# Bias tables of the neighbourhood attention: laid out on the host and loaded by one plain transfer

## The chip, the cores and the metric

The kernel runs on one core of a Trainium2 chip. The metric is device time in microseconds (us) of one execution, as the median of several runs. Engines: PE multiplies matrices (PEld loads its stationary operand), DVE and ACT work on vectors, POOL (GpSimd) does small vector work and issues some transfers, SP issues most transfers.

## The reference, cut to what matters

Three layers over 256 tokens of width 1024: an attention layer with an MLP, a retention layer with an MLP, and a hybrid attention layer. The first layer has eight heads of window attention (a) and eight of neighbourhood attention (b). Tokens form 4 rows of 64 columns; a query sees, in every row, 16 columns around its own, with a bias per head, row distance and column distance:

```
cstart = jnp.clip(qc - kw // 2, 0, GRID_W - kw)
col_valid = (kc[None, :] >= cstart[:, None]) & (kc[None, :] < cstart[:, None] + kw)
col_idx = jnp.clip(kc[None, :] - qc[:, None] + NA_KW - 1, 0, 2 * NA_KW - 2)
...
bias = rpb_f[:, row_idx[None, :, None], col_idx[:, None, :]]
s = jnp.where(col_valid[:, None, :], s + bias, -jnp.inf)
```

## The kernel before, in words

All weights stream from HBM once, in 1 MB pieces on SP's queue. Each is split into two fp32r parts: ACT copies the rounded part (whi, L246), DVE subtracts it (wlo, L251), and PE multiplies three times. The activations are split in the same way.

The order of instructions on every engine is written by a planner that runs while the kernel is built. The code consists of tasks (generators). Each operation names its engine and an estimated cost; a task goes on when its engine, its inputs and its buffers are free by these estimates, and among the tasks that are ready the one of the lowest priority number is first. The real engines then run their instructions in that order and wait on semaphores for each other. So a step that is taken out of one engine's plan can move other steps, if they stood behind it.

The stage in question is the first attention layer (`_even`, from about 10 to 120 us). Its projections are five panels, qa, ka, qb, kb and vb, of 48 matmuls each. Between the matmuls of a panel lie the heads (`even_head`): PE makes 128x256 scores of two halves; DVE adds a table and takes the row minimum in a custom instruction (L273); ACT takes exponentials (L246); DVE adds the sink to the denominator (den, L251), inverts it (L288) and scales p (tensor_scalar, L259); PE transposes p (L336); ACT and DVE split the result (ph, pl); PE multiplies by v (PV).

The eight (a) heads use a table that DVE makes for each from distances in the tile conste (tab, L259). The eight (b) heads use the tile tb: 128 partitions (2 grid rows x 64 query columns) by 8 heads by 6 rows by 64 key columns. A head for token half t reads 256 of the 384 columns, from 128 - 128t.

tb is filled by the task `bias_tables`, spawned with a delay of 30 (BIAS) and low priority (5). Two transfers on POOL's queue (`pdma`, L302, planned at 1.04 each) read the host's rows, which are repeated 64 times in HBM, with a pitch of one element less than a row, so that partition q gets the row shifted by q. That makes 6144 runs of 64 floats. Columns outside the window then hold other values, and four POOL additions (`ptt`, L293) of 128x768 elements add a mask of 0 and -1e30, which came with conste. The plan gives each 0.0021 us per element and 0.1. At the end the task fires the event "tb", for which the planner holds back head 8, the first (b) head; that head also waits for the panels qb, kb and vb. Other work on POOL in this stage is the inverse square root as a power (`rsqrt`, L298) of st (the norms of q and k heads), r and rm.

Tiles of the stage come from two pools (`Pools`): those whose size is a multiple of 512 bytes from one, the others from the second. conste has 448 columns (1792 bytes), and lies in the second.

Of the kernel before, what the change touches and what calls it, by code (L numbers as in the profile page):

```python
# [11 lines left out]
ALU = mybir.AluOpType  # L12
# [3 lines left out]
P = 128  # L16
# [5 lines left out]
NEG = -1e30  # L22
# [6 lines left out]


K_ID, K_CM, K_CC, K_SS, K_MAIN = 0, 128, 384, 512, 640
K_DIST, K_WM, K_EVEN = 640, 1024, 1088
K_DPOS, K_DNEG, N_CONST = 1088, 1472, 1856

A_ORDER = [0, 4, 1, 5, 2, 6, 3, 7]

# [1 line left out]
def vap(ap, dims):  # L38

    return bass.AP(ap.tensor, ap.offset, [ap.ap[0]] + [list(d) for d in dims])  # L40
# [24 lines left out]
class Kernel:  # L65
# [801 lines left out]
    def _even(self, pool):  # L867
        nc, aps, cols = self.nc, self.aps, self.cols
        self.res["qn"] = 2
        self.hb = self.EB  # L870
        const = pool.tile([P, K_EVEN - K_MAIN], F32, name="conste")
        nc.sync.dma_start(const, aps["const"][:, K_MAIN:K_EVEN])
        dist, wmask = const[:, K_DIST - K_MAIN:K_DIST - K_MAIN + 384], const[:, K_WM - K_MAIN:K_WM - K_MAIN + 64]

        gg = pool.tile([P, 2], F32, name="gg")
        for i, (cq, ck) in enumerate(((C_QA, C_KA), (C_QB, C_KB))):
# [3 lines left out]
        tb = pool.tile([P, 8, 6 * 64], F32, name="tb")  # L880

        def bias_tables():

            rp = aps["rpb"]
            for r2 in range(2):
                src = bass.AP(rp.tensor, rp.offset + r2 * 48 * 64 * P + 63, [[P - 1, 64], [64 * P, 48], [1, 64]])
                self.pdma(tb[r2 * 64:(r2 + 1) * 64].rearrange("p h (j k) -> p (h j) k", k=64), src)
            yield 15.0
            wm = vap(wmask, [[0, 12], [1, 64]])
            for h in range(0, 8, 2):  # L890
                tv = tb[:, h:h + 2].rearrange("p h (j k) -> p (h j) k", k=64)
                yield from self.ptt(tv, tv, wm, ALU.add)
            self.fire("tb", at=self._last(self.ready, tb, "T"))
        self.spawn(bias_tables(), self.BIAS, self.LOW)

        def qk_norm(ps, t, nh):
# [737 lines left out]
def _pack(w, panels, kmajor=False):  # L1634

    kt = w.shape[0] // P
    blocks = []
    idx = [(c, g) for c in range(len(panels)) for g in range(kt // 4)]
    if kmajor:
        idx = [(c, g) for g in range(kt // 4) for c in range(len(panels))]  # L1640
    for c, g in idx:
        a, b = panels[c]
        blk = w[g * 512:(g + 1) * 512, a:b].reshape(4, P, b - a).transpose(1, 0, 2)
        blocks.append(np.ascontiguousarray(blk).reshape(-1))
    return np.concatenate(blocks)


def _uniform(n, w=512):
    return [(i, i + w) for i in range(0, n, w)]


def _columns(v):
    return np.ascontiguousarray(np.asarray(v).reshape(-1, P).T)


def _constants():
    c = np.zeros((P, N_CONST), np.float32)
    p = np.arange(P)[:, None]
    c[:, K_ID:K_ID + P] = np.eye(P)
    d = np.abs(np.arange(384)[None, :] - P - p)  # L1660
    c[:, K_DIST:K_DIST + 384] = np.where(d <= 128, d, 1e30)
    c[:, K_CM + P:K_CM + 2 * P] = np.where(np.arange(P)[None, :] <= p, 0.0, NEG)
    qc = p % 64
    st = np.clip(qc - 8, 0, 48)
    kc = np.arange(64)[None, :]
    c[:, K_WM:K_WM + 64] = np.where((kc >= st) & (kc < st + 16), 0.0, NEG)
    diff = np.arange(384)[None, :] - P - p
    c[:, K_DPOS:K_DPOS + 384] = np.maximum(diff, 0)
    c[:, K_DNEG:K_DNEG + 384] = np.maximum(-diff, 0)
    inv = np.power(np.float32(10000.0), -np.arange(32, dtype=np.float32) * np.float32(2.0) / np.float32(64))  # L1670
    for t in range(NT):
        ang = ((p + t * P).astype(np.float32) * inv[None, :].astype(np.float32)).astype(np.float64)
        co, si = np.cos(ang), np.sin(ang)
        c[:, K_CC + t * 64:K_CC + (t + 1) * 64] = np.concatenate([co, co], 1)
        c[:, K_SS + t * 64:K_SS + (t + 1) * 64] = np.concatenate([-si, si], 1)
    return c


def _layout(inputs):
    i = {k: np.asarray(v) for k, v in inputs.items()}  # L1680
    f = {}
    f["x"] = i["x"][0]
    f["mem"] = i["mem_2"][0]
    cols = np.zeros((P, N_COLS), np.float32)
    for base, v in ((G_ATTN, i["attn_norm_e"][0]), (G_MLP0, i["mlp_norm"][0]), (G_MLP1, i["mlp_norm"][1]),
                    (G_RET, i["ret_norm_o"][0]), (G_GN, i["ret_gn_o"][0]), (G_IN, i["g_in_2"][0]),
                    (G_MEM, i["g_mem_2"][0])):
        t = _columns(v)
        cols[:, base:base + t.shape[1]] = t
    for base, n in ((C_QA, "q_norm_a"), (C_KA, "k_norm_a"), (C_QB, "q_norm_b"), (C_KB, "k_norm_b")):  # L1690
        cols[:, base] = np.tile(i[n][0], 2)
    cols[:, C_SINK:C_SINK + 8] = i["sink_a"][0][None, :]
    cols[:, C_DEC:C_DEC + 8] = i["decay_fwd_o"][0][None, :]
    cols[:, C_DEC + 8:C_DEC + 16] = i["decay_bwd_o"][0][None, :]
    f["cols"] = cols
    f["const"] = _constants()
    rpb = np.zeros((2, 8, 6, P), np.float32)
    for r2 in range(2):
        rpb[r2, :, :, 48:79] = i["rpb_b"][0][:, 5 - r2:11 - r2, :]
    f["rpb"] = np.tile(rpb, 64)  # L1700
    w = i["w_in_e"][0]
    qa = w[:, :512].reshape(D, 8, 64)[:, A_ORDER].reshape(D, 512)
    f["w_in_e"] = _pack(np.concatenate([qa, w[:, 512:]], 1),
                        [(0, 512), (512, 768), (768, 1280), (1280, 1792), (1792, 2304)])
    wo = i["w_out_e"][0]
    oa = wo[:512].reshape(8, 64, D)[A_ORDER].reshape(512, D)
    f["w_out_e"] = _pack(np.concatenate([oa, wo[512:]], 0), _uniform(D), kmajor=True)
    w = i["w_in_o"][0]
    parts = []
    for hp in range(4):  # L1710
        parts += [w[:, hp * 256:(hp + 1) * 256], w[:, D + hp * 256:D + (hp + 1) * 256],
                  w[:, 2 * D + hp * 512:2 * D + (hp + 1) * 512], w[:, 4 * D + hp * 512:4 * D + (hp + 1) * 512]]
    f["w_in_o"] = _pack(np.concatenate(parts, 1), _uniform(6 * D))
    f["w_out_o"] = _pack(i["w_out_o"][0], _uniform(D), kmajor=True)
    for l in range(2):
        f[f"w_mlp_in{l}"] = _pack(i["w_mlp_in"][l], _uniform(4 * D))
        f[f"w_mlp_out{l}"] = _pack(i["w_mlp_out"][l], _uniform(D), kmajor=True)
    f["w_mem"] = _pack(i["w_mem_kv_2"][0], _uniform(D))
    w = i["w_in_2"][0]
    MQ, MK, MV, MG, DQ, DK, DV, DG, IQ, IK, XQ, XG, GL = (0, 512, 1024, 1536, 2048, 2560, 3072, 3584, 4096, 4608,  # L1720
                                                         4680, 5192, 5704)
    full = lambda o: (o, o + 512)
    f["w_in_2"] = _pack(w, [full(IQ), (IK, IK + 328), (XQ + 256, XQ + 512), full(XG), full(MQ), full(MK), full(MV),
                            full(GL + 2048), full(GL + 2560), full(DQ), full(DK), full(DV), full(MG),
                            full(GL), full(GL + 512), full(DG), full(GL + 1024), full(GL + 1536)])
    f["b_merge"] = i["b_merge_2"][0]
    f["w_up"] = np.concatenate([_pack(i[n][0], _uniform(D)) for n in ("w_up_cross_2", "w_up_moba_2", "w_up_dsa_2")])
    f["w_out_2"] = _pack(i["w_out_2"][0], _uniform(D), kmajor=True)
    f["g_final"] = i["g_final_2"]
    return {k: np.ascontiguousarray(v, dtype=np.float32) for k, v in f.items()}  # L1730
# [20 lines left out]
```

## Time and profile before

| | us |
|---|---|
| median of 3 runs | 1014.18 (1013.54 to 1014.5) |
| the profiled execution | 1014.55 |
| its span | 1012.8 |

| engine | busy us | share of the span |
|---|---|---|
| PE | 1000.0 | 99% |
| PEld | 860.1 | 85% |
| DVE | 689.5 | 68% |
| ACT | 536.1 | 53% |
| POOL | 39.5 | 4% |

The span begins with the first instruction and ends with the last. An engine is busy while an instruction of its own lies on it; an instruction that is held by something else counts as busy too. PE's ends are modelled, so starts are the better measure there. The granted clock is the share of full speed that the chip allowed PE: 1.0 is 2.4 GHz, 0.5 is 1.2 GHz. A row of the order of time gives start, length, engine, line, operation, the tiles (out<-in), the shape and the count; a bracket at its end gives the idle time before it and what ended that.

### The profile page before, as it was taken

To read this page: it belongs to the slowest core of one execution; us is meant where nothing else is said; L and a number is where in the kernel's file an instruction comes from. 1 tells how busy PE (TensorE), PEld (TensorE's weight loads), DVE (VectorE), ACT (ScalarE), POOL (GpSimd) and SP (SyncE) were. 2 spreads that over 40 slices of the span, in tenths; PEclk is the share of its full clock that TensorE was granted. 3 is DMA by queue.
4 is the path that set the end of the run, shared out by engine and by line. 5 is a ranking of instruction groups with operands and counts; after the bars stand their busy time and mean duration, and the time that the engine had idled before them with its cause. 6 is when DMAs were issued, how large, how long until landed. Compare 5 with 4: busy or idle time off the path is not lost.

```text
span 1012.8 us, 14238 instructions
## 1 busy us (share of the span) xinstructions
PE 1000.0 (99%) x5602; PEld 860.1 (85%) x5602; DVE 689.5 (68%) x1133; ACT 536.1 (53%) x817; POOL 39.5 (4%) x44
## 2 busy tenths in 40 slices
PE   9989999999999999999999999999999999999997
PEld 7878889999998888888889999998878788888885
DVE  6997667555556977777667545556769756576774
ACT  7766646444445655656446444445554553454453
POOL 1340000000000000000000000000100000000000
PEclk9989999999999999999999999999999999999999
DMA  9734245555554544443545555553625435543531
GB/s 333 231 112 159 84 166 203 178 202 182 197 204 153 195 166 155 172 171 129 205 166 191 187 206 172 203 207 112 213 83 172 161 136 195 193 172 128 195 125 42
DMA packets 27108, 173.66 MB, mean 171 GB/s; under 512 B 3168, under 2 KB 3424, under 8 KB 7584
## 3 DMA queue, kind: packets, MB, share of 16 engines
q1 hardware_dynamic: 25344, 168.05, 47.2%
q0 software_dynamic: 1120, 4.06, 1.7%
q8 instruction: 44, 0.72, 0.3%
q10 hardware_dynamic: 576, 0.64, 0.2%
q14 instruction: 24, 0.20, 0.1%
HBM read 171.69 MB, written 1.05 MB: 171 GB/s over the span
## 4 chain that ended last, share of the span: by engine, by line
PE 95%; DVE 2%; DMA 1%; ACT 1%; issue 0%; POOLq 0%; ACTq 0%; DVEq 0%
PE bank L326 91%; PE bank L336 4%; DMA x<-in_x 1%; DVE p L273 1%; DVE tab L259 0%; DMA cols<-in_cols 0%; ACT p L246 0%; DVE pl L251 0%; DVE p L259 0%; DVE den L251 0%; DVE wlo L251 0%; DVE st L283 0%; DVE qn L251 0%; ACT whi L246 0%; ACT nraw L246 0%
## 5 line engine op out<-in xcount | busy, mean ns | idle before, releaser
L251 DVE TENSOR_TENSOR wlo<-raw,whi 128x1024 fp32r<-128x1024 f32 (+1 forms) x324 | 384.9, 1191 | 187.9 <-ACT whi L246 183.0
L246 ACT ACTIVATE whi<-raw 128x1024 fp32r<-128x1024 f32 (+1 forms) x324 | 333.3, 1032 | 239.5 <-PE bank L326 233.8
L326 PE MATMUL bank<-whi,xT 128*128 128x512 f32 (+2 forms) x1184 | 378.7, 390 | 0.7 <-ACT whi L246 0.4
L326 PEld LDWEIGHTS bank<-whi,xT 128*128 128x128 f32 x1184 | 221.1, 189 | 45.7 <-issue 3.0
L326 PE MATMUL bank<-wlo,xT 128*128 128x512 f32 (+2 forms) x592 | 227.1, 384 | 0.0
L326 PE MATMUL bank<-xT,whi 128*128 128x256 f32 x1024 | 182.1, 280 | 0.0
L326 PEld LDWEIGHTS bank<-xT,whi 128*128 128x128 f32 x1024 | 157.3, 187 | 1.1
L326 PE MATMUL bank<-xT,wlo 128*128 128x256 f32 x512 | 142.9, 279 | 0.0
L326 PEld LDWEIGHTS bank<-wlo,xT 128*128 128x128 f32 x592 | 112.0, 189 | 18.8
L326 PE MATMUL bank<-whi,hh 128*128 128x512 f32 x256 | 100.3, 392 | 0.0
L326 PE MATMUL bank<-whi,hl 128*128 128x512 f32 x256 | 99.8, 390 | 0.0
L326 PE MATMUL bank<-wlo,hh 128*128 128x512 f32 x256 | 99.6, 389 | 0.0
L326 PEld LDWEIGHTS bank<-xT,wlo 128*128 128x128 f32 x512 | 96.2, 188 | 0.0
L326 PEld LDWEIGHTS bank<-whi,hl 128*128 128x128 f32 x256 | 48.0, 188 | 10.4
L326 PEld LDWEIGHTS bank<-wlo,hh 128*128 128x128 f32 x256 | 48.1, 188 | 9.5
L326 PEld LDWEIGHTS bank<-whi,hh 128*128 128x128 f32 x256 | 48.1, 188 | 9.3
L246 ACT ACTIVATE p<-p,nm 128x256 f32<-128x256 f32 (+1 forms) x64 | 30.2, 473 | 27.1 <-DVE nm L273 26.9
L251 DVE TENSOR_TENSOR h<-h 128x512 f32<-128x512 f32 x32 | 22.0, 688 | 18.1 <-ACT h L246 18.1
L246 ACT ACTIVATE h<-bank 128x512 f32<-128x512 f32 x32 | 18.8, 587 | 28.6 <-PE bank L326 28.6
L246 ACT ACTIVATE hh<-h 128x512 fp32r<-128x512 f32 x32 | 20.2, 632 | 19.6 <-DVE h L251 19.6
L251 DVE TENSOR_TENSOR hl<-h,hh 128x512 fp32r<-128x512 f32 x32 | 22.0, 688 | 11.2 <-ACT hh L246 11.2
L326 PE MATMUL bank<-whi,uh 128*128 128x512 f32 x64 | 25.2, 393 | 0.0
(241 smaller groups left out, 1117.3 us busy)
## 6 DMA issues: line engine op xcount, KB each, us to landing
raw<-in_w_mlp_in SPq DMA_DIRECT2D x32, 1024.0 KB, 4.7
raw<-in_w_mlp_out SPq DMA_DIRECT2D x32, 1024.0 KB, 4.8
raw<-in_w_in SPq DMA_DIRECT2D x32, 1024.0 KB, 4.9
raw<-in_w_in_o SPq DMA_DIRECT2D x24, 1024.0 KB, 4.7
raw<-in_w_out_o SPq DMA_DIRECT2D x8, 1024.0 KB, 4.7
raw<-in_w_in_e SPq DMA_DIRECT2D x6, 1024.0 KB, 5.5
raw<-in_w_up SPq DMA_DIRECT2D x6, 1024.0 KB, 4.9
raw<-in_w_mem SPq DMA_DIRECT2D x4, 1024.0 KB, 4.8
```

The source lines that it names most:

```text
L246: self.nc.scalar.activation(out, in_, func, scale=scale, **kw)
L251: self.nc.vector.tensor_tensor(out, a, b, op=op)
L273: self.nc.vector.tensor_tensor_reduce(out, a, b, scale, init, op0, op1, acc)
L326: self.nc.tensor.matmul(out, lhsT, rhs, start=start, stop=stop, skip_group_check=shared)
L336: self.nc.tensor.transpose(out, in_, self.ident)
```

## The change

The host makes the whole tile tb, mask included, in the order in which it lies in SBUF: 128 rows of 3072 floats. One transfer on POOL's queue loads it. The additions, the mask in conste and the wait of 15 in the task are gone; the event "tb" fires 8 after the issue. conste becomes 384 columns (1536 bytes) and so lies in the first pool.

```
-K_DIST, K_WM, K_EVEN = 640, 1024, 1088
-K_DPOS, K_DNEG, N_CONST = 1088, 1472, 1856
+K_DIST, K_EVEN = 640, 1024
+K_DPOS, K_DNEG, N_CONST = 1024, 1408, 1792
...
-        dist, wmask = const[:, K_DIST - K_MAIN:K_DIST - K_MAIN + 384], const[:, K_WM - K_MAIN:K_WM - K_MAIN + 64]
+        dist = const[:, K_DIST - K_MAIN:K_DIST - K_MAIN + 384]
...
         def bias_tables():
-
-            rp = aps["rpb"]
-            for r2 in range(2):
-                src = bass.AP(rp.tensor, rp.offset + r2 * 48 * 64 * P + 63, [[P - 1, 64], [64 * P, 48], [1, 64]])
-                self.pdma(tb[r2 * 64:(r2 + 1) * 64].rearrange("p h (j k) -> p (h j) k", k=64), src)
-            yield 15.0
-            wm = vap(wmask, [[0, 12], [1, 64]])
-            for h in range(0, 8, 2):
-                tv = tb[:, h:h + 2].rearrange("p h (j k) -> p (h j) k", k=64)
-                yield from self.ptt(tv, tv, wm, ALU.add)
-            self.fire("tb", at=self._last(self.ready, tb, "T"))
+            self.pdma(tb.rearrange("p h k -> p (h k)"), aps["rpb"])
+            yield 8.0
+            self.fire("tb", at=self.now)
...
+def _bias(rpb):
+
+
+    r2, qc = np.arange(P)[:, None, None] // 64, np.arange(P)[:, None, None] % 64
+    row, kc = np.arange(6)[None, :, None], np.arange(64)[None, None, :]
+    first = np.clip(qc - 8, 0, 48)
+    inside = (kc >= first) & (kc < first + 16)
+    vals = rpb[:, 5 - r2 + row, np.clip(kc - qc + 15, 0, 30)].transpose(1, 0, 2, 3)
+    return np.where(inside[:, None], vals, np.float32(NEG)).reshape(P, 8 * 384)
...
-    rpb = np.zeros((2, 8, 6, P), np.float32)
-    for r2 in range(2):
-        rpb[r2, :, :, 48:79] = i["rpb_b"][0][:, 5 - r2:11 - r2, :]
-    f["rpb"] = np.tile(rpb, 64)
+    f["rpb"] = _bias(i["rpb_b"][0])
```

## Rows read from the trace of the kernel before

**Rows 1.** The page: busy time by engine, granted clock in 40 slices.
```profile
PE 1000.0 (99%) x5602; PEld 860.1 (85%) x5602; DVE 689.5 (68%) x1133; ACT 536.1 (53%) x817; POOL 39.5 (4%) x44
...
PEclk9989999999999999999999999999999999999999
```

**Rows 2.** The page: the chain that ended last, share of the span by line.
```profile
PE bank L326 91%; PE bank L336 4%; DMA x<-in_x 1%; DVE p L273 1%; DVE tab L259 0%; DMA cols<-in_cols 0%; ACT p L246 0%; DVE pl L251 0%; DVE p L259 0%; DVE den L251 0%; DVE wlo L251 0%; DVE st L283 0%; DVE qn L251 0%; ACT whi L246 0%; ACT nr
```

**Rows 3.** Waits of PE, whole span: us in total, times, longest.
```profile
PE bank L336 <- DVE p L259: 3.2, 1, 3.2
...
PE bank L336 <- DVE den L251: 0.5, 1, 0.5
```

**Rows 4.** Windows of 1 us: length, busy time by engine, granted clock, DMA.
```profile
60.00:61.00 1.00, 0.00 (x0) 0.00 (x0) 1.00 (x7) 0.71 (x3) 0.00 (x0) 0.50 0.00 0
...
66.00:67.00 1.00, 1.00 (x7) 0.86 (x6) 1.00 (x2) 0.36 (x1) 0.00 (x0) 0.83 0.00 0
```

**Rows 5.** PE in order of time, around its long wait.
```profile
57.55 0.40 PE L326 MATMUL bank<-whi,xT 128*128 128x512 f32 x1
61.13 1.09 PE L336 MATMUL bank<-const,p 128*128 128x128 f32 x4 [3.18 <-DVE p L259]
...
66.55 0.28 PE L326 MATMUL bank<-ph,vah 128*128 128x256 f32 x1
```

**Rows 6.** POOL in order of time: the four mask additions.
```profile
52.45 7.38 POOL L293 TENSOR_TENSOR tb<-tb,conste 128x768 f32<-128x768 f32 x4
```

**Rows 7.** DVE in order of time, 54 to 69 us.
```profile
54.60 3.58 DVE L259 TENSOR_SCALAR tab<-conste 128x384 f32<-128x384 f32 x2
58.10 1.75 DVE L251 TENSOR_TENSOR den<-den,es 128x2 f32<-128x2 f32 x1
59.77 0.47 DVE L273 CUSTOM_DVE_ANT_0 p<-bank,tab,nsink 128x256 f32<-128x256 f32 x1
...
60.64 0.61 DVE L259 TENSOR_SCALAR p<-p,den 128x256 f32<-128x256 f32 x2
61.17 0.47 DVE L273 CUSTOM_DVE_ANT_0 p<-bank,tab,nsink 128x256 f32<-128x256 f32 x1
...
64.32 0.61 DVE L259 TENSOR_SCALAR p<-p,den 128x256 f32<-128x256 f32 x2
...
68.59 0.69 DVE L251 TENSOR_TENSOR pl<-bank,ph 128x512 fp32r<-128x512 f32 x1 [1.32 <-ACT ph L246]
```

**Rows 8.** The chain in order of time: start, us on the chain, what.
```profile
42.85 0.07 DVE den L251
...
44.46 0.26 DVE tab L259
```

**Rows 9.** PE in order of time: scores before the wait, work at full clock.
```profile
55.93 1.13 PE L326 MATMUL bank<-kTa,qTa 64*128 64x256 f32 x4
...
67.26 0.60 PE L336 MATMUL bank<-const,p 128*128 128x128 f32 x4
67.62 0.48 PE L326 MATMUL bank<-whi,xT 128*128 128x512 f32 x1
...
70.45 0.28 PE L326 MATMUL bank<-ph,vah 128*128 128x256 f32 x1
```

**Rows 10.** POOL in order of time, 35 to 75 us.
```profile
35.78 2.92 POOL L302 DMA_DIRECT2D tb<-in_rpb  x2
40.12 1.65 POOL L298 TENSOR_TENSOR st<-st,mhalf 128x8 f32<-128x8 f32 x1 [1.43 <-DVE st L261]
...
72.81 2.49 POOL L298 TENSOR_TENSOR st<-st,mhalf 128x8 f32<-128x8 f32 x1 [12.98 <-DVE st L261]
```

**Rows 11.** Line 302, transfers issued on POOL: ns min/median/max, first and last start.
```profile
L302 POOL DMA_DIRECT2D tb<-in_rpb x2: 1365/1460/1554, 35.8 to 37.3; - x2
...
L302 POOL DMA_DIRECT2D gf<-in_g_final x1: 533/533/533, 928.8 to 928.8; - x1
```

**Rows 12.** The tile tb: who reads it, ns min/median/max, first and last start.
```profile
L273 DVE CUSTOM_DVE_ANT_0 p<-bank,tb x16: 403/419/425, 93.9 to 111.6; 128x256 f32<-128x256 f32 x16
```

More of the change, by code (lines that the diff above doesn't have):

```diff
@@ L1662, in _constants @@
     c[:, K_CM + P:K_CM + 2 * P] = np.where(np.arange(P)[None, :] <= p, 0.0, NEG)
[L1663 to L1666, printed above, removed]
     diff = np.arange(384)[None, :] - P - p
```

## The prediction

> **What bounds the kernel now.** I read the page first, then the chain that ended last, then who PE waited for, and from there the order of time around the one long wait.
>
> PE is busy 99% of the span, and the granted clock is 90% or more in every slice but the third, 50.6 to 76 us [rows 1]. In the chain two PE lines hold 95%, and the only transfers in it are those of the start, x and cols [rows 2]. So PE's own work is the bound almost everywhere, and a change on POOL can only pay where PE waits. In the list of PE's waits one stands out: 3.2 us, one time, for a tensor_scalar of DVE on p [rows 3]. It ends at 61.13 us, ahead of four transposes; the matmul before had started at 57.55 [rows 5]. The windows of one microsecond show a second price: the granted clock is 0.50 in 60 to 61 and 0.83 in 66 to 67 [rows 4]. It fell to its lower level (1.2 GHz) while PE idled, and came back only after PE had worked some 5 us.
>
> Why was DVE late? In that stretch POOL runs the four mask additions back to back, 52.45 to 59.83 [rows 6]. Exactly there three small DVE instructions are long: two tab (from 54.60, 3.58 us together) and one den (58.10, 1.75 us); the next one starts at 59.77 [rows 7]. In the chain a tab elsewhere takes 0.26 us and a den 0.07 [rows 8]. The den is a sum of two numbers per partition; it ends at 59.85, with the last addition. So it didn't work, it was held, until POOL let go.
>
> **The change part by part.**
>
> *The four additions go.* DVE, from the first tab to the instruction behind den, takes 59.77 - 54.60 = 5.17 us. At the price of elsewhere it is 2 x 0.26 + 0.07 = 0.59, so DVE gets 4.58 us back. The p that PE waited for is the pair at 60.64 [rows 7], ready when PE goes on at 61.13; it moves to about 56.5. Its scores don't hold it: PE makes them before those of the next head, at 55.93 [rows 9]. PE is free for the transposes at about 57.8, so over 1 us remains as cover, and the wait is gone entirely.
>
> *What PE gains.* I count from start to start, since matmuls overlap. Before: the last weight matmul starts at 57.55, the PV matmul behind the disturbed stretch at 66.55 [rows 5], 9.00 us. Between them stand eight transposes and nine 512-wide matmuls. At the full clock four transposes take 67.62 - 67.26 = 0.36, and the twelve matmuls from 67.62 to 70.45 take 2.83, 0.236 each [rows 9]. So the same work needs 0.24 (the matmul at 57.55 itself) + 2 x 0.36 + 9 x 0.236 = 3.08, and PE gains 9.00 - 3.08 = 5.9 us. The wait is 61.13 - 57.55 - 0.24 = 3.3 of it, the half clock 2.6.
>
> *What is late next.* PE gains more than DVE, so DVE's lead shrinks. The scores started at 55.93 end at 57.06 [rows 9]; the custom instruction at 61.17 reads them and can't start before 57.1, so from there DVE is only some 4.1 us earlier. The tightest hand-off is the pair of p at 64.32, done by 64.9 [rows 7], for the transposes at 67.26 [rows 9]: 2.3 us of slack. It becomes 2.3 - (5.9 - 4.1) = 0.5 us. Still positive, so I take no new wait. Soon after, DVE idles 1.32 us for ACT's ph, at 68.59 [rows 7]; that is room in which it catches up with PE. Behind that PE is the chain to the end [rows 2], so the 5.9 us stay.
>
> *The clock.* With no idle time at 58 to 61 nothing of the kind that preceded the fall is left; I take full clock throughout.
>
> *The DMA.* Two transfers on POOL's queue, 1.37 and 1.55 us to issue, become one of 128 rows. No issue of the trace has 12 KB rows; the nearest is the 128-row load of gf, 0.53 us [rows 11]. I take 0.6; the ends are 0.5 and 2.9 (the two together). Both lie inside POOL's idle time: the two took 2.92 us from 35.78, and then POOL still stood idle 1.43 us for DVE before the st at 40.12 [rows 10]. So the term is zero at either end; if the cover were gone, what goes beyond it would fall on that st (rival d). Landing doesn't count either: the tables are first read at 93.9 [rows 12], over 50 us after the issue, and at about 88 after the change. The tile's bytes are the same, and no load of weights ends a wait in the chain [rows 2].
>
> *Order and queues.* The planner writes every engine's order, so I ask what stood behind the removed steps on POOL. The st behind the DMAs and the st behind the masks waited for DVE, 1.43 and 12.98 us [rows 10]; POOL held neither. SP's and ACT's queues carry nothing of the change but a conste that is narrower by 64 columns. The event that lets the second half of the heads start fires earlier, but those heads also need projections that end long after it. I cost the order at zero; if it did move, one hand-off of the size of PE's other waits (0.5 us, rows 3) would be the price, either way.
>
> *Addresses.* conste falls into the other pool, so tiles of this stage shift by 1.5 KB. No row compares two layouts. The nearest is the custom instruction on the eight tables, at eight places of the tile: 403 to 425 ns over 16 [rows 12]. 22 ns on each of the some 15 DVE instructions ahead of the tight hand-off is 0.3 us, either way. I take zero.
>
> Sum: 5.9 us. The profiled execution took 1014.55 (span 1012.8 and 1.75 around it), 0.37 over the median of 1014.18. So it would be 1008.6 in that execution, and 1008.3 against the median.
>
> **The rivals.**
>
> (a) *The wait goes, the half clock stays.* The clock would fall for a reason other than the idle time. For it: one case is all that the trace has. Against: the clock is full in every later slice [rows 1], where PE doesn't wait. Then only 3.3 us are gained: 1010.9. Chance 7%.
>
> (b) *The wait moves to the next hand-off.* The 0.5 us of slack left above is worked out without ACT's share and without any wait on the way from one engine to the next. If DVE is late at four hand-offs by 0.5 us each (the size of PE's wait for den, rows 3), 2 us of the gain go: 1010.3. Chance 6%.
>
> (c) *The long DVE instructions have another cause*, or something behind them holds PE just as long: 1014.2. For it: the two tab read conste, as the additions do, so that the tile might be at fault. Against: den doesn't read it and is held too. Chance 5%.
>
> (d) *Slower: the plain transfer holds POOL.* The place is POOL's queue at 35.78: the st at 40.12 stands behind the issue [rows 10], and DVE's qn, with the heads behind it in order, behind that st. An issue of up to 40.12 - 35.78 = 4.3 us loses nothing; beyond it each microsecond goes to DVE and on to PE, which in that part already waits once for DVE's den [rows 3]. From 10.2 us on, the gain of 5.9 is lost; at 12.5 the kernel is 8.2 - 5.9 = 2.3 us slower: 1016.5. Against: no issue that I read took over 1.55 us [rows 11]. Chance 4%.
>
> The Trainium skill speaks for this rival ("SBUF — State Buffer", section "SBUF: two separate sides"): the descriptors of a transfer issued from GpSimd are written by GpSimd itself, through a port that it shares with DVE, and they wait while DVE runs its fast fp32 copies; it advises another queue. By that rule the one transfer could be held where DVE is busy nearly all the time, and the sum would lose whatever goes beyond the idle time. No run here shows such a hold so far: the issues of 1.37 and 1.55 us stood beside DVE's work.
>
> **How the numbers follow.** The forecast has 78%, (a) 7, (b) 6, (c) 5, (d) 4. What a measurement of this kernel can tell from no change is about 0.2%, 2 us. Faster by more than that: 78 + 7 + 6 = 91%; within it: 5%; slower: 4%. The range begins at 1007.5 (the forecast, less 0.3 for the addresses and 0.5, half of the spread of the runs before, 1013.54 to 1014.5) and goes to 1011.0, so that (a) and (b) are inside.
>
> **What would show it.** Right: tab at about 0.26 and den at 0.07 everywhere in the chain; no wait of PE of 3 us for p; a granted clock of 1.00 in every window from 50 to 80; the first table read near 88; everything behind shifted by the same 5.9 us. Wrong would be a wait of PE over 1 us between 56 and 75, a clock of 0.5 there without idle time ahead of it, a den or tab over 1 us, or an issue over 4 us on POOL.

## The result, and the profile after

| | before | after |
|---|---|---|
| median, us | 1013.86 (1013.2 to 1014.5, 4 runs) | 1008.37 (1008.18 to 1009.06, 4 runs) |
| ratio | | 0.9947 (95%: 0.993 to 0.9964) |
| the profiled execution | 1014.55 | 1008.18 |
| its span | 1012.8 | 1006.4 |

The kernel is 5.5 us faster, where 5.9 were forecast. That the time itself is only 0.1 us from the predicted 1008.3 is partly luck: the forecast started from the median of three runs of before, 1014.18, and the median of four is 0.3 lower, which makes up for most of the 0.4 us that the gain fell short.

First the waits of PE over the whole span (us in total, times, longest). The 3.2 us for DVE's p, first in [rows 3], are gone; nothing new stands in their place.

```profile
PE bank L831 <- DVE vx L824: 1.1, 1, 1.1
PE bank L336 <- DVE den L251: 0.5, 1, 0.5
PE bank L326 <- ACT whi L246: 0.4, 2, 0.3
PE bank L336 <- ACT p L246: 0.2, 1, 0.2
```

Then DVE in order of time (... stands for rows left out). The two tab take 0.61 us together and the den 0.15, where they took 3.58 and 1.75 [rows 7]; from the first tab to the instruction behind den it is 54.74 - 54.13 = 0.61 us, before 5.17.

```profile
54.13 0.61 DVE L259 TENSOR_SCALAR tab<-conste 128x384 f32<-128x384 f32 x2
54.66 0.15 DVE L251 TENSOR_TENSOR den<-den,es 128x2 f32<-128x2 f32 x1
54.74 0.47 DVE L273 CUSTOM_DVE_ANT_0 p<-bank,tab,nsink 128x256 f32<-128x256 f32 x1
...
55.61 0.60 DVE L259 TENSOR_SCALAR p<-p,den 128x256 f32<-128x256 f32 x2
56.13 0.47 DVE L273 CUSTOM_DVE_ANT_0 p<-bank,tab,nsink 128x256 f32<-128x256 f32 x1
...
58.37 0.69 DVE L251 TENSOR_TENSOR nraw<-bank,cols 128x512 f32<-128x512 f32 x1 [0.33 <-PE bank L336]
...
59.58 0.61 DVE L259 TENSOR_SCALAR p<-p,den 128x256 f32<-128x256 f32 x2
```

PE over the same work. The last weight matmul starts at 57.07, the transposes follow at once, and the PV matmul starts at 60.23: 3.16 us for what took 9.00 [rows 5].

```profile
57.07 0.39 PE L326 MATMUL bank<-whi,xT 128*128 128x512 f32 x1
57.30 0.60 PE L336 MATMUL bank<-const,p 128*128 128x128 f32 x4
...
60.23 0.28 PE L326 MATMUL bank<-ph,vah 128*128 128x256 f32 x1
...
60.94 0.60 PE L336 MATMUL bank<-const,p 128*128 128x128 f32 x4
```

Windows of 1 us (length, busy time of PE, PEld, DVE, ACT, POOL, granted clock, DMA share, GB/s): PE is busy throughout, and the clock is full where it was 0.50 and 0.83 [rows 4].

```profile
58.00:59.00 1.00, 1.00 (x8) 0.87 (x6) 0.67 (x3) 1.00 (x4) 0.00 (x0) 1.00 0.00 0
...
60.00:61.00 1.00, 1.00 (x9) 0.96 (x8) 1.00 (x6) 1.00 (x2) 0.00 (x0) 1.00 0.00 0
...
66.00:67.00 1.00, 1.00 (x7) 0.82 (x6) 1.00 (x4) 0.73 (x2) 0.34 (x1) 1.00 0.40 164
```

And POOL: one issue of 0.72 us in place of two of 2.92 together [rows 10], then 3.64 us idle, and no additions.

```profile
35.30 0.72 POOL L302 DMA_DIRECT2D tb<-in_rpb  x1
39.66 1.66 POOL L298 TENSOR_TENSOR st<-st,mhalf 128x8 f32<-128x8 f32 x1 [3.64 <-DVE st L261]
```

The two spans differ by 6.4 us. Of these the stretch gives 9.00 - 3.16 = 5.84. Another 0.48 was there before it: the matmul of 57.55 stands at 57.07. That belongs to the start of the single execution and not to the change; in the experiments below the same matmul stands anywhere from 56.69 (the one with SP's queue) to 57.94 (the one with the old addresses). Behind the stretch the two traces run in parallel: 370.00 us of PE in the 370 us from 130 before, and the same in the 370 us from 124 after. A table at the end of the experiments gives the time behind this matmul for every kernel.

### The profile page after: what moved, and what is told of

Its sections match the earlier page's. It is cut to its first block, busy times and chain, and to the rows that moved or that the text cites. A ratio compares the mean times of both kernels' runs of the same rounds, so it can differ in the third digit from the quotient of the medians.

```text
span 1006.4 us, 14233 instructions
## 1 busy us (share of the span) xinstructions
PE 997.3 (99%) x5602; PEld 858.6 (85%) x5602; DVE 684.8 (68%) x1133; ACT 536.0 (53%) x817; POOL 30.4 (3%) x39
## 3 DMA queue, kind: packets, MB, share of 16 engines
HBM read 171.65 MB, written 1.05 MB: 172 GB/s over the span
## 4 chain that ended last, share of the span: by engine, by line
PE 97%; ACT 1%; DVE 1%; DMA 1%; issue 0%; SPq 0%; POOL 0%; DVEq 0%; POOLq 0%
PE bank L326 93%; PE bank L336 4%; DMA raw<-in_w_in_e 1%; DVE p L273 0%; ACT p L246 0%; ACT whi L246 0%; SPq L388 0%; ACT nraw L246 0%; ACT u L246 0%; DVE x L251 0%; DVE st L283 0%; ACT qn L246 0%; DVE qn L251 0%; DVE tab L259 0%; POOL r L298 0%
```

## The experiments

**The additions alone, put back on the changed kernel.** They add zeros from const, a tile that the held instructions don't use.

```
             self.pdma(tb.rearrange("p h k -> p (h k)"), aps["rpb"])
-            yield 8.0
-            self.fire("tb", at=self.now)
+            yield 15.0
+            wm = vap(self.const[:, K_CM:], [[0, 12], [1, 64]])
+            for h in range(0, 8, 2):
+                tv = tb[:, h:h + 2].rearrange("p h (j k) -> p (h j) k", k=64)
+                yield from self.ptt(tv, tv, wm, ALU.add)
+            self.fire("tb", at=self._last(self.ready, tb, "T"))
```

> The changed kernel with its one plain transfer, and with four POOL additions of 128x768 put back at their old place. They add zeros from another tile (const), so neither conste nor a mask is touched. My theory (POOL's additions hold DVE, each to its end): the two tab and the den are long again (5.2 us from the first tab to the instruction behind den), PE waits 3.2 us for p, the clock falls to 0.5, and the time is that of before, 1014.0 (1013.3 to 1014.7). Rival 1 (the gain came from the transfer, the plan or the addresses): 1008.4, no wait. Rival 2 (the two tab were slow because they read conste, which the additions read too): only den is long, DVE loses 1.6 us instead of 4.6, PE waits under 0.5 us, 1008.4 to 1009.5.

Measured: 1014.03, ratio to before 1.0003 (0.9993 to 1.0012). All of the gain is gone again. DVE, in order of time, is as in [rows 7], to the hundredth in the den:

```profile
54.57 3.59 DVE L259 TENSOR_SCALAR tab<-conste 128x384 f32<-128x384 f32 x2
58.08 1.75 DVE L251 TENSOR_TENSOR den<-den,es 128x2 f32<-128x2 f32 x1
59.75 0.47 DVE L273 CUSTOM_DVE_ANT_0 p<-bank,tab,nsink 128x256 f32<-128x256 f32 x1
```

So the additions alone carry the effect, and rival 2 of this experiment, a conflict over conste, falls. The windows show a difference in the clock:

```profile
60.00:61.00 1.00, 0.00 (x0) 0.00 (x0) 1.00 (x7) 0.73 (x3) 0.00 (x0) 1.00 0.00 0
61.00:62.00 1.00, 0.89 (x6) 0.86 (x7) 1.00 (x4) 1.00 (x5) 0.00 (x0) 0.83 0.00 0
62.00:63.00 1.00, 1.00 (x6) 0.90 (x5) 1.00 (x7) 1.00 (x5) 0.00 (x0) 0.50 0.00 0
...
65.00:66.00 1.00, 1.00 (x6) 0.78 (x5) 1.00 (x6) 1.00 (x2) 0.00 (x0) 0.96 0.00 0
```

Here it fell only when PE was at work again. By the windows of 0.83 and 0.96 the half clock lasted from about 61.7 to 65.1. The work from the transposes (61.11) to the PV matmul (65.78) took 4.67 us; at full clock it takes 60.23 - 57.30 = 2.93 (after). So the half clock cost 1.7 us in this execution, against 5.42 - 2.93 = 2.5 in that of before.

**The additions alone, taken from the kernel before.** Its two transfers, its conste and its wait stay; the mask is left out of the neighbourhood heads.

```
-            for h in range(0, 8, 2):
-                tv = tb[:, h:h + 2].rearrange("p h (j k) -> p (h j) k", k=64)
-                yield from self.ptt(tv, tv, wm, ALU.add)
-            self.fire("tb", at=self._last(self.ready, tb, "T"))
+            self.fire("tb", at=self.now)
```

> The kernel before with its two transfers of short runs, its wide conste and its wait of 15, but without the four additions; it leaves out the mask of the neighbourhood heads. My theory: the whole gain, 1008.4 (1007.9 to 1009.1), no wait of PE for p of 3 us, clock 1.00 from 50 to 80 us, although the two transfers hold POOL for 2.9 us as before. Rival 1 (transfer, plan, addresses): 1013.9.

Measured: 1008.37, ratio 0.9946 (0.9931 to 0.9961), the median of the changed kernel to the hundredth. The two transfers still held POOL for 2.90 us, with 1.44 us of idle time behind them. The form of the transfer and the host's layout are worth nothing by themselves here; they are what lets the additions go.

**The same mask in sixteen short additions.**

```
-            wm = vap(wmask, [[0, 12], [1, 64]])
-            for h in range(0, 8, 2):
-                tv = tb[:, h:h + 2].rearrange("p h (j k) -> p (h j) k", k=64)
-                yield from self.ptt(tv, tv, wm, ALU.add)
+            wm = vap(wmask, [[0, 3], [1, 64]])
+            for h in range(8):
+                for c in range(2):
+                    tv = tb[:, h, c * 192:(c + 1) * 192].rearrange("p (j k) -> p j k", k=64)
+                    yield from self.ptt(tv, tv, wm, ALU.add)
```

> The kernel before with the mask added in sixteen instructions of 128x192 in place of four of 128x768; the same elements, POOL busy for some 8 us as before. My theory (DVE is held to the end of the POOL instruction that runs, then gets its turn): a held instruction waits 0.5 us at most instead of 1.9. Six DVE instructions in SBUF stand from the first tab to the p that PE needs, so p comes at most 3 us later than without additions, and with the 1.3 us of cover PE waits 0.3 to 1.5 us, too short for the clock to fall: 1008.8 to 1010.5. Rival (POOL and DVE share a rate, or DVE gets no turn before POOL is done): DVE loses what it lost, PE waits 3 us, 1013.9 to 1014.8.

Measured: 1009.23, ratio 0.9955 (0.9938 to 0.9971). POOL, then DVE, then PE in order of time:

```profile
51.89 9.52 POOL L293 TENSOR_TENSOR tb<-tb,conste 128x192 f32<-128x192 f32 x16
```

```profile
54.03 1.01 DVE L259 TENSOR_SCALAR tab<-conste 128x384 f32<-128x384 f32 x2
54.97 0.55 DVE L251 TENSOR_TENSOR den<-den,es 128x2 f32<-128x2 f32 x1
55.44 0.47 DVE L273 CUSTOM_DVE_ANT_0 p<-bank,tab,nsink 128x256 f32<-128x256 f32 x1
...
56.31 1.05 DVE L259 TENSOR_SCALAR p<-p,den 128x256 f32<-128x256 f32 x2
```

```profile
61.61 0.55 PE L336 MATMUL bank<-const,p 128*128 128x128 f32 x3 [0.21 <-DVE p L259]
```

POOL works longer than with four additions (9.52 against 7.38 us), and yet DVE loses about a sixth of what it lost before: 55.44 - 54.03 = 1.41 us from the first tab to the instruction behind den, 0.80 over the 0.61 of the changed kernel; before it was 4.56 over. The pair of p behind it is held too, 1.05 us for 0.60. So it isn't POOL's amount of work that counts, but how long the one instruction lasts that DVE meets. PE waits 0.21 us, one time, and the clock stays full.

**The wait kept, but filled with work for PE.** In the head whose p came late:

```
         yield ("op", "T", [], [p])
+        if j == 4:
+            zero = self.vx[1][:, :P].bitcast(mybir.dt.bfloat16)
+            for _ in range(30):
+                self.nc.tensor.matmul(ps[:, :256], zero[:, :P], zero[:, :256], start=True, stop=True)
```

> The kernel before with 30 bf16 matmuls of zeros (256 columns, about 0.107 us each at full clock) put in front of the four transposes for which PE waited 3.2 us; their result is overwritten by the transposes. DVE is held as before. My theory (the clock fell because PE idled): the clock stays at 1.00 from 58 to 67 us, PE's wait for p is under 0.4 us, and the half clock's share of the gain comes back: 1013.9 - 2.6 = 1011.3 (1010.8 to 1011.9). Rival (the clock falls there for a reason other than idle time): granted clock 0.5 again, 1013.9 or more.

Measured: 1012.11, ratio 0.9978 (0.9968 to 0.9987): a gain of 2.0 us, where 2.6 were expected; the time is 0.2 us above the expected range. PE in order of time, and two windows:

```profile
57.70 0.40 PE L326 MATMUL bank<-whi,xT 128*128 128x512 f32 x1
57.93 3.45 PE L722 MATMUL bank<-vx 128*128 128x256 bf16 x30
61.22 0.80 PE L336 MATMUL bank<-const,p 128*128 128x128 f32 x4
...
64.36 0.28 PE L326 MATMUL bank<-ph,vah 128*128 128x256 f32 x1
```

```profile
60.00:61.00 1.00, 1.00 (x11) 0.89 (x10) 1.00 (x7) 0.55 (x3) 0.00 (x0) 1.00 0.00 0
...
63.00:64.00 1.00, 1.00 (x6) 0.83 (x5) 1.00 (x4) 1.00 (x5) 0.00 (x0) 1.00 0.00 0
```

The transposes come as late as ever, but the clock never falls. So the idle time is what brought the fall, and the two parts of the gain can be told apart: 2.0 us of clock, by the medians, and 1012.11 - 1008.37 = 3.7 us of wait, between medians that were not taken side by side. In the trace the stretch takes 64.36 - 57.70 = 6.66 us, 3.50 over the 3.16 of the changed kernel. That the clock's share is below the 2.6 worked out beforehand agrees with the additions put back, where it was 1.7: the profiled execution of before had a dear fall.

**The same additions, 18 us later in the plan.**

```
-            yield 15.0
+            yield 33.0
             wm = vap(wmask, [[0, 12], [1, 64]])
```

> The kernel before with the same four additions planned 18 us later, behind the first st of the kb panel (one behind it, three behind the second st); one scalar instruction of DVE changes its place by this. POOL does the same work, the place differs. My theory (an addition costs only what DVE's hold takes beyond the slack of the next hand-off to PE): no wait of 3 us at 58 to 61. In the new place DVE has wlo and other SBUF instructions that are held, some 4 us in all, but from there on it idles in between, and the nearest hand-off (qn for the transposes) has 1.7 us of slack; PE waits 0 to 2 us, 1008.4 to 1011. Rival (four additions cost what they cost, wherever they are): 1014.

Measured: 1008.69, ratio 0.9952 (0.9935 to 0.9968). POOL, then DVE in order of time:

```profile
69.62 1.85 POOL L293 TENSOR_TENSOR tb<-tb,conste 128x768 f32<-128x768 f32 x1
...
73.26 2.29 POOL L293 TENSOR_TENSOR tb<-tb,conste 128x768 f32<-128x768 f32 x1
75.50 1.86 POOL L293 TENSOR_TENSOR tb<-tb,conste 128x768 f32<-128x768 f32 x1
77.30 2.85 POOL L293 TENSOR_TENSOR tb<-tb,conste 128x768 f32<-128x768 f32 x1
```

```profile
70.44 1.06 DVE L261 TENSOR_SCALAR st<-st,em 128x8 f32<-128x8 f32 x1
...
75.57 2.87 DVE L251 TENSOR_TENSOR wlo<-raw,whi 128x1024 fp32r<-128x1024 f32 x1
78.36 2.87 DVE L251 TENSOR_TENSOR wlo<-raw,whi 128x1024 fp32r<-128x1024 f32 x1
```

DVE is held nearly as much as before: the two wlo take 5.66 us together, where two in a row take 2.35 elsewhere in the kernel before, and st 1.06 for 0.23; 4.1 us in all. PE has no wait from it in its list of waits. Four additions cost 5.5 us or nothing that can be told, by their place. Here the hold seems to go both ways. The addition from 75.50 keeps its 1.86 us and the wlo beside it is long; the next addition starts at 77.30, when that wlo gets its turn, and takes 2.85.

**The old addresses.** conste takes 448 columns again, 384 of them loaded.

```
-        const = pool.tile([P, K_EVEN - K_MAIN], F32, name="conste")
+        const = pool.tile([P, 448], F32, name="conste")[:, :K_EVEN - K_MAIN]
```

> The changed kernel with conste as a tile of 448 columns again, of which 384 are loaded, so that it lies in the second pool and all tiles of the stage have their old addresses. My theory (addresses cost nothing): 1008.4 (1007.9 to 1008.9), DVE's lengths as in the changed kernel. Rival (the shift by 1.5 KB is part of the gain): 0.3 us or more above that.

Measured: 1008.79, ratio 0.9953 (0.9938 to 0.9968). The medians can't decide: 1008.79 lies in the range for no effect and also over the 0.3 us of the rival. The traces can. The weight matmul before the transposes stands at 57.94, 0.87 us later than in the changed kernel, and the last matmul of the program at 1000.11, 0.85 later than 999.26. So the whole excess of this execution was there before the stretch, and the addresses cost nothing in it. The reads of the tables take 401 to 425 ns, in the changed kernel 403 to 425.

**The table transfer on SP's queue.**

```
-            self.pdma(tb.rearrange("p h k -> p (h k)"), aps["rpb"])
+            nc.sync.dma_start(tb.rearrange("p h k -> p (h k)"), aps["rpb"])
```

> The changed kernel with its table transfer on SP's queue in place of POOL's. The Trainium skill (SBUF - State Buffer, section SBUF: two separate sides) advises this, because GpSimd writes descriptors through the port that it shares with DVE. My theory (the issue on POOL, 0.72 us, and the landing, 9.3 us after it, are covered; the tables are read 52 us later): no change, 1008.4 (1007.9 to 1009.1); landing perhaps shorter. Rival 1 (DVE's hold of POOL's descriptors costs something): up to 0.5 us faster. Rival 2 (the transfer holds up weight loads behind it on SP's queue): slower by more than 0.5 us, with waits of ACT whi on raw.

Measured: 1009.19, ratio 0.9956 (0.9941 to 0.9971): the two intervals overlap, but the median is 0.1 us above the expected range and 0.8 over the changed kernel, more than the 0.5 of rival 2. What that rival named doesn't show: from 28 to 75 us no wait of ACT for raw stands in its list, and from the weight matmul before the transposes (56.69) to the last one (998.86) this trace is as long as that of the changed kernel, to 0.02 us. The profiled execution took 1008.31, though, and the three others 1009.11 to 1009.32; no trace shows what they spent more. The transfer landed after 9.3 us; on POOL's queue it took 9.3 too, and 7.9 with the old addresses. So the advice that the expectation takes from the Trainium skill shows no gain here, neither in the landing nor in the time.

**Eight additions in place of four**, on the kernel with the additions put back.

```
-            for h in range(0, 8, 2):
+            for h in [0, 2, 4, 6] * 2:
```

> The kernel with the additions put back (zeros from const, one plain transfer), now with eight of them back to back, 52.4 to about 67.2 us, on POOL. My theory (each holds the next DVE instruction that lies wholly in SBUF, to its end): after den, also the pair of p, the second den, and the third tab are held, one per addition. The p that PE waits for comes about 3 us later than with four, PE waits some 6 us, and later hand-offs wait again: 1017 to 1021. Rival (DVE was held by only the first ones, whatever their number): 1014.

Measured: 1016.54, ratio 1.0027 (1.0017 to 1.0037), 2.5 us over the kernel with four, where 3 to 7 were expected; the forecast was too high. DVE in order of time:

```profile
60.58 2.92 DVE L259 TENSOR_SCALAR p<-p,den 128x256 f32<-128x256 f32 x2
...
64.82 0.37 DVE L251 TENSOR_TENSOR den<-den,es 128x2 f32<-128x2 f32 x1
65.12 0.35 DVE L259 TENSOR_SCALAR tab<-conste 128x384 f32<-128x384 f32 x1
...
66.65 0.93 DVE L259 TENSOR_SCALAR p<-p,den 128x256 f32<-128x256 f32 x2
```

The pair of p is held by 2.3 us, as expected; PE waits 3.94 and 1.27 us for it in two pieces, 5.2 in all, and the half clock lasts from 59 to 69. But den and the next pair lose only 0.2 and 0.3 us, and tab nothing, although POOL is at work until 67.15: they came near the end of an addition, or between two. I had counted one full hold for each addition. What an instruction loses is what is left of the addition that it meets.

**All profiled executions, without their start.** From the weight matmul before the transposes (57.07 in the changed kernel) to the last matmul of the program, start to start, in us:

| kernel | from | to | length | over the changed one |
|---|---|---|---|---|
| changed | 57.07 | 999.26 | 942.19 | |
| no additions | 57.23 | 999.40 | 942.17 | -0.02 |
| old addresses | 57.94 | 1000.11 | 942.17 | -0.02 |
| SP's queue | 56.69 | 998.86 | 942.17 | -0.02 |
| additions later | 57.57 | 999.75 | 942.18 | -0.01 |
| sixteen additions | 56.98 | 999.87 | 942.89 | 0.70 |
| wait filled | 57.70 | 1003.39 | 945.69 | 3.50 |
| additions put back | 57.52 | 1004.81 | 947.29 | 5.10 |
| before | 57.55 | 1005.62 | 948.07 | 5.88 |
| eight additions | 57.49 | 1008.11 | 950.62 | 8.43 |

The first five agree to 0.02 us, so the plain transfer, its queue, the addresses and the late additions are worth nothing in these executions. The wait alone is 3.50, and the half clock comes on top of it: 5.88 - 3.50 = 2.4 in before and 5.10 - 3.50 = 1.6 with the additions put back, close to the 2.5 and 1.7 that the rows above gave.

## Why the prediction was right, step by step

*Additions gone, DVE gets 4.58 us back.* Measured 5.17 - 0.61 = 4.56. Shown from both sides, by the additions put back and by those taken from the kernel before.

*The wait goes, 3.3 us.* It went. By the kernel that fills the wait it was worth 3.5 us in the trace and 3.7 in the medians.

*The half clock goes, 2.6 us.* The mechanism is shown, the size was that of one execution. Three profiles of kernels with the wait have it at different places; in before and with the additions put back it cost 2.5 and 1.7 us, and 2.0 by the medians. It differs among the runs of the kernel before, too: of the 19 beside the filled wait, the ten with a mean granted clock of 0.994 or 0.995 took 1013.85 to 1015.11 us, the nine with 0.996 to 0.998 took 1012.34 to 1014.09. So this term was 0.6 us too high, and the wait, 3.3 for 3.5, 0.2 too low; together they are the 0.4 us by which the forecast of 5.9 lies over the 5.5 that came.

*Nothing is late next, with 0.5 us left at the tightest hand-off.* The pair of p starts at 59.58 and is done by 60.2, the transposes begin at 60.94: 0.7 us. One reason that I gave was wrong: the custom instruction at 61.17 before, 56.13 now, doesn't read the scores of the group before it on PE (55.93 before, 55.44 now), and starts while that group still runs. DVE makes one tab for each (a) head, and the eighth and last comes only at 57.61; so the custom instruction at 56.13 belongs to an earlier head, and the last group of scores is read from 60.17 on.

```profile
55.44 1.13 PE L326 MATMUL bank<-kTa,qTa 64*128 64x256 f32 x4
```

```profile
57.61 0.35 DVE L259 TENSOR_SCALAR tab<-conste 128x384 f32<-128x384 f32 x1
...
60.17 0.48 DVE L273 CUSTOM_DVE_ANT_0 p<-bank,tab,nsink 128x256 f32<-128x256 f32 x1
```

So the bound of 4.1 us wasn't there: DVE kept its 4.6, which alone would leave 2.3 - (5.9 - 4.6) = 1.0 us. It then idled 0.33 us for PE at 58.37, which the sum didn't have, and 0.7 was left. That 0.5 was nearly right is luck.

*The transfer at zero.* Issue 0.72 us where I took 0.6, 3.64 us of idle time behind it, first read of the tables at 87.5 (I said near 88). Rival (d) never had its condition of 4.3 us.

*Order and addresses at zero.* Behind the stretch the traces run in parallel, and the kernel with the old addresses takes the same time there to 0.02 us.

Rival (a), the clock, fell to the filled wait; (b) fell to the list of PE's waits, which has no new one; (c) fell to the additions put back and to those taken from the kernel before.

What holds DVE is settled as far as that it is POOL's additions, one by one, and only for some instructions: those of DVE that read PSUM for one input, as the custom one and pl, ran at full speed beside them, here beside the additions of before, which start at 52.45:

```profile
53.19 0.47 DVE L273 CUSTOM_DVE_ANT_0 p<-bank,tab,nsink 128x256 f32<-128x256 f32 x1
...
53.99 0.68 DVE L251 TENSOR_TENSOR pl<-bank,ph 128x512 fp32r<-128x512 f32 x1
```

The Trainium skill has this as a rule ("SBUF — State Buffer", section "Who interferes with whom"): POOL shares a port pair with DVE, and a DVE instruction that runs in a fast two-port mode, or reads two inputs from SBUF while POOL's reads SBUF too, excludes a POOL instruction for its whole length, and the other way round, whichever comes first. The held ones (tab, p, den, st, wlo) and the addition stretched to 2.85 us agree; the mode in which tab, p and st ran is in no trace. One row doesn't agree: beside a power on POOL in the changed kernel, which reads SBUF, stands a wlo with two SBUF inputs at its usual 1.21 us.

```profile
49.52 1.64 POOL L298 TENSOR_TENSOR st<-st,mhalf 128x8 f32<-128x8 f32 x1 [8.21 <-DVE den L288]
```

```profile
50.39 1.21 DVE L251 TENSOR_TENSOR wlo<-raw,whi 128x1024 fp32r<-128x1024 f32 x1
```

So not every POOL instruction holds DVE for its whole length; why wasn't tried.

## What to carry to other kernels

An engine with 4% busy time can still set the kernel's time (here 7.4 us of additions cost 5.5 us), if its instructions hold another engine that has a late hand-off: look for short instructions with long rows, and for what ends at the same moment on another engine. Before such work is taken out, moving it to a place where the held engine isn't late, or cutting it into short instructions, gave nearly all of the gain here (5.0 and 4.9 of 5.5 us). And a wait of PE as long as this one is to be priced with the half clock behind it, as a range, since that part differs from one execution to the next.

## What the runs showed of the hardware that was not expected

- After the same idle time of 3.2 us the granted clock fell at different moments: in the kernel before while PE idled (0.76 in 59 to 60), with the additions put back only after PE had gone on (1.00 in 60 to 61, 0.50 in 62 to 63).
- One transfer of 128 rows of 12 KB landed 9.3 us after its issue on either queue, and 7.9 after it with the old addresses, hardly sooner than the two of 256-byte runs in before (8.4 to 10.5). Its issue on POOL took 0.72 us where theirs took 2.92.
- A power on 128x8 elements on POOL (1.64 us) didn't hold a wlo beside it; additions of 128x192 (0.60 us each) did hold den and p.
